# Up projections of three feed-forward stages as 2x2 block products with seven multiplications

## The chip, the cores and the metric

One core of one Trainium2 chip runs the whole program. The metric is the device time of one execution in microseconds (us). Three runs of the kernel before took 2185.04 to 2186.0 us, median 2185.47.

## What is computed

Input is one sequence of 512 tokens with 1024 features, float32 throughout. Two hybrid layers (attention, convolution and retention side by side) are followed by a third block with differential attention and a state space layer. Each of the three ends in a feed-forward stage, and only these three stages change:

```python
# hybrid layer, twice: w_up is 1024 x 4096, w_down 4096 x 1024
h = rms_norm(x, g_mlp_pre)
f = jnp.square(jax.nn.relu(h @ w_up)) @ w_down
return x + rms_norm(f, g_mlp_post)

# second block: w_up is 1024 x 5632 (gate and value), w_down 2816 x 1024
hn = rmsnorm(h, norm2_gain[i])
up = causal_dwconv(hn @ w_up[i], conv_w[i], conv_b[i])     # 3 taps along the tokens
gate, val = jnp.split(up, 2, axis=-1)
h = h + (jax.nn.silu(gate) * val) @ w_down[i]
```

## The kernel before

Every float32 operand of a matmul is split into a high part (rounded to the matmul's float32r type) and a low part, the remainder, and every product is three matmuls: high by high, high by low, low by high (mm3, L863, for up projections; t_part, L911, for down projections). A matmul contracts 128 rows and has a 128x128 stationary operand and up to 512 moving columns.

Weights are streamed (class Stream, L729) in chunks of 128x1024 in the order that stream_spec (L60) lists. A chunk is loaded by a DMA on SP's queue into one of NR = 4 raw buffers (wraw, pool wr). prep_to (L748) casts it to whi and subtracts to get wlo, each in one of NW = 4 buffers (pools wh and wl). The cast may go to ACT or DVE, the subtraction to DVE or POOL. The rest of SBUF is a pool sp of 79 - 2*NR - 4*NW = 55 tiles of 128x512 (L829). PSUM has two pools of four banks, psp and pss (L832, L833).

An up unit (f_unit, L890) makes 128 features for all 512 tokens: 8 blocks of the contraction, 24 matmuls of 512 columns into one bank. The input is the transposed, normed activation, hhi and hlo (to_hT, L985). The first four units of a stage go through f_split (L896): first the 256 columns of tokens 0 to 255 of all four, then the other 256, while the last token tiles are still being normed and transposed (mid_start, L1049). After a unit its evacuation runs: relu squared and a split into fhi and flo in mlp (relu2, L1454), the three-tap convolution on ACT and DVE, SiLU, gate times value and a split in ffn2 (unit, L2012). The down projection of four such units (down, L1483) is 96 matmuls of 512 columns, and DVE adds each bank to an accumulator tile (acc in mlp; in ffn2 the residual X itself). mlp (L1444) has 8 groups of four units; ffn2 (L2006) has 22 pairs of a gate and a value unit, four pairs to a down projection. finish_mlp (L1504) does the last down projection, the norm, the residual and the first half of the next stage's norm.

The order of the instructions is not the program's. Class Trace (L400) records every instruction with a due time and a cost by a formula (cost, L682), and order (L443) puts them on the engines' queues as a list schedule: each engine takes the ready instruction that is due first, up to WINDOW = 25160 ns ahead, if buffers are free (room, L609). Weight chunks are due PREPV = 15000 ns ahead of their use, evacuations EVV = 5000 ns ahead of the end of their unit. Where an instruction may go to two engines, a bias decides: Trace.sub (L648) passes an index into BIAS (L404), and POOL's end is counted as that many ns later. wbias is 2 (-4449 ns, in favour of POOL) outside the feed-forward stages and 3 (-1000 ns) in them; the index 1 means 100000 ns, so that POOL is never taken. The queues' order is fixed when the program is built.

Beside mlp of the first layer a side task (ssm_params, L1525) computes tables of the state space layer, mostly on POOL, and stores them.

Of the kernel before, what the change touches and what calls it, by code (L numbers as in the profile page):

```python
# [17 lines left out]
P = 128  # L18
# [28 lines left out]
def mlp_groups():  # L47
    return [(4 * g, 4) for g in range(NG1)]


def ffn2_groups():
    n = DFF2 // 128
    return [(k, min(4, n - k)) for k in range(0, n, 4)]
# [6 lines left out]
def stream_spec():  # L60
    out = []
    for l in range(LAYERS):
# [12 lines left out]
        gs = mlp_groups()  # L75
        for g, (k0, n) in enumerate(gs):
            out += [f_chunk("w_up", l, 128 * (k0 + i)) for i in range(n)]
            if g:
                out += down_chunks("w_down", l, *gs[g - 1])
        out += down_chunks("w_down", l, *gs[-1])  # L80
# [19 lines left out]
    gs = ffn2_groups()  # L100
    for g, (k0, n) in enumerate(gs):
        for i in range(n):
            out.append(f_chunk("w_up_2", 0, 128 * (k0 + i)))
            out.append(f_chunk("w_up_2", 0, DFF2 + 128 * (k0 + i)))
        if g:
            out += down_chunks("w_down_2", 0, *gs[g - 1])
    out += down_chunks("w_down_2", 0, *gs[-1])
# [117 lines left out]
class View:  # L225
    """A view of a tile that is traced before the tile is placed."""
# [103 lines left out]
class DramView(View):  # L330
    """A view of a tile in DRAM: taken as a whole."""
# [20 lines left out]
class Pool:  # L352
    """Equal slots, which the order of instructions deals out to tiles. Each is a pool of one buffer."""
# [46 lines left out]
class Trace:  # L400
    """Records instructions with the time by which each is wanted, orders them, and issues them."""
# [246 lines left out]
    def sub(self, out, a, b, bias=1):  # L648
# [3 lines left out]
        return self.add(alts, (out, a, b), {"op": ALU.subtract})  # L652
# [119 lines left out]

class Side:
# [35 lines left out]
class Builder:  # L809
# [3 lines left out]
    NR, NW = 4, 4  # L813
# [6 lines left out]
    def __init__(self, tc, ctx, A, out):  # L820
# [17 lines left out]
        self.wbias = 2  # L838

# [23 lines left out]
    def mm3(self, ps, w, a, start, stop):  # L863
        nc = self.nc
        (whi, wlo), (ahi, alo) = w, a
        nc.tensor.matmul(ps, whi, ahi, start=start, stop=False)
        nc.tensor.matmul(ps, whi, alo, start=False, stop=False)
        nc.tensor.matmul(ps, wlo, ahi, start=False, stop=stop)
        self.tick(3 * ahi.n * 0.422)
# [72 lines left out]
    # ---------------------------------------------------------------- norms  # L942
# [42 lines left out]
    def to_hT(self, t, hs):  # L985
        nc = self.nc
        for h in range(2):
# [4 lines left out]
            self.split(ps.rearrange("p (k n) -> p k n", k=4), self.hhi[sl], self.hlo[sl])  # L992
# [66 lines left out]
    # ---------------------------------------------------------------- attention helpers  # L1059
# [41 lines left out]
    def v_pack(self, src):  # L1101
        """V of six heads, each as 64 columns of high parts and 64 of low parts."""
# [11 lines left out]
    def pv_pair(self, h, pts, V, y):  # L1114
        """One head's output, from the products with the high and the low parts of V below each other."""
# [19 lines left out]
    def rows(self, third):  # L1135
        """Room for the four rows of blocks of a lower triangle."""
# [3 lines left out]
    def p_split(self, parts):  # L1140
        """High and low parts by blocks of keys: 512, 384 and twice 256 columns, the last with a block of zeros."""
# [58 lines left out]
    # ---------------------------------------------------------------- conv module  # L1200
# [48 lines left out]
    # ---------------------------------------------------------------- retention  # L1249
# [87 lines left out]
    # ---------------------------------------------------------------- hybrid layer  # L1337
    def hybrid(self, l):
# [69 lines left out]
        # output projection and residual  # L1408
# [14 lines left out]
        self.side.drain()  # L1423
        self.finish(lambda t: (p0[t],), 4, W_OUT_KS, mix, X, gpost, gpre)
# [18 lines left out]
    # ---------------------------------------------------------------- MLP  # L1443
    def mlp(self, l, X):  # L1444
        nc = self.nc
        groups = mlp_groups()
        self.wbias = 3
        if l == 0:
            self.side.add(self.ssm_params())
        acc = [None] * NT  # L1450
        f = {}
        last_g = len(groups) - 1

        def relu2(m):  # L1454
            def ev(ps):
                r = self.s2()
                nc.vector.tensor_scalar(r, ps, 0.0, None, op0=ALU.max)
                hi, lo = self.s2(F32R, "fhi"), self.s2(F32R, "flo")
                nc.scalar.activation(hi, r, AF.Square)
                nc.scalar.activation(r, r, AF.Square)  # L1460
                nc.vector.tensor_tensor(lo, r, hi.bitcast(F32), op=ALU.subtract)
                f[m] = (hi, lo)
            return ev
        lhs = lambda k, t0, t1: tuple(z[:, t0:t1] for z in f[k])
        for g, (k0, n) in enumerate(groups):
            if g == 0:
                self.f_split([relu2(i) for i in range(n)], self.mid_start((1, 3)))
                gpost = self.load_gain(4 * l + 3)
                nxt = 4 * (l + 1) if l + 1 < LAYERS else 8
                gpre = self.load_gain(nxt)  # L1470
            else:
                for i in range(n):
                    self.f_unit(relu2(k0 + i))
                self.down(groups[g - 1], lhs, acc, f, g == 1)
        xd = [[self.dp.tile(F32, f"xd{l}_{t}_{h}", [P, 512]) for h in range(2)] for t in range(NT)]

        def store(t):
            for h in range(2):
                nc.sync.dma_start(out=xd[t][h], in_=X[t][h])
        self.finish_mlp(groups[-1], lhs, acc, X, gpost, gpre, store)  # L1480
        self.xd = xd

    def down(self, grp, lhs, acc, f, first):  # L1483
# [20 lines left out]
    def finish_mlp(self, grp, lhs, acc, X, gpost, gpre, store):  # L1504
        nc = self.nc
        k0, n = grp
        nch = n // 2
        ks = list(range(k0, k0 + n))
        ws = [self.ws.take() for _ in range(2 * nch)]
        hs = {}  # L1510
        for t in range(NT):
            for h in range(2):
                ps = self.ps()
# [7 lines left out]
            store(t)  # L1521
        self.pending = hs

    # ---------------------------------------------------------------- SSM parameters
# [158 lines left out]
    # ---------------------------------------------------------------- SSM  # L1683
# [84 lines left out]
    # ---------------------------------------------------------------- differential attention  # L1768
# [84 lines left out]
    def second(self):  # L1853
# [139 lines left out]
        hs = {}  # L1993
        for t in range(NT):
# [11 lines left out]
    def ffn2(self, X):  # L2006
        nc = self.nc
        f, tg = {}, {}
        self.wbias = 3
        cw, cb = PV["convw2"][0], PV["convb2"][0]  # L2010

        def unit(i, val):  # L2012
            c = i + (22 if val else 0)

            def ev(ps):
                t = self.s2(name="cv")
                w = [self.pvt[:, cw + 3 * c + j:cw + 3 * c + j + 1] for j in range(3)]
                nc.scalar.activation(t, ps, AF.Identity, scale=w[2], bias=self.pvt[:, cb + c:cb + c + 1])
# [61 lines left out]
```

## Time and profile before

| | before |
|---|---|
| runs | 2185.04, 2185.47, 2186.0 us |
| span of the profiled execution | 2185.0 us |
| feed-forward stage of layer 0 (290 to 666) | 376 us |
| feed-forward stage of layer 1 (947 to 1305) | 358 us |
| feed-forward stage of the second block (1812 to the end) | 373 us |
| the rest | 1078 us |

The page gives no time of the profiled execution apart from its span, which lies within 0.05 us of the fastest run. Nearly every instruction carries the line 642, where the recorded instructions are issued, so the profile is read by the names of tiles: wraw, whi and wlo are weights, hhi and hlo the input of the up projections, fhi and flo the input of the down projections, ps a PSUM bank, acc or X an accumulator, cv a convolved unit. The duration of a matmul in the trace is longer than the distance from one start to the next, since matmuls overlap; the distance of starts is what counts. The same holds for DVE and ACT to a lesser degree.

### The profile page before, as it was taken

What the parts mean: (1) busy time and instruction counts of PE and PEld (TensorE: products, weight loads), DVE (VectorE), ACT (ScalarE), POOL (GpSimd) and SP (SyncE); (2) the same over time, 40 slices, a digit from 0 to 9 for tenths busy, and PEclk for the clock granted to TensorE, in tenths of its full rate; (3) what the DMA queues carried; (4) which work ended last, traced back from release to release, by engine and by line L of the source; (5) the groups of instructions that cost most, each with busy time, mean ns of one, the idle gap of its engine ahead of it and who ended that gap; (6) DMA issues with size and microseconds to landing.
All of it is one profiled execution on the core that took longest, in us unless ns stands there. A gap on an engine that the chain in (4) does not pass through costs nothing. (4 is left out here: it accounts for less than half of the span.)

```text
span 2185.0 us, 27033 instructions
## 1 busy us (share of the span) xinstructions
PE 2065.8 (95%) x9964; PEld 1711.6 (78%) x9964; DVE 1395.2 (64%) x2131; ACT 928.5 (42%) x1521; POOL 745.5 (34%) x858
## 2 busy tenths in 40 slices
PE   7789989899999799989999998999999999999999
PEld 7777878778888777788888877677777788888887
DVE  6999596344457999573444464379888646655545
ACT  3267544232234267454222344456578324433332
POOL 3663357980004663210000115764643431000000
PEclk9999999999999999999999999999999999999999
DMA  5223233332333224133332346222224533333222
GB/s 176 80 78 123 87 116 109 128 127 87 97 114 97 87 68 135 49 107 97 96 97 77 115 133 201 79 80 68 92 82 135 169 96 97 97 96 97 87 87 77
DMA packets 85556, 225.16 MB, mean 103 GB/s; under 512 B 10416, under 2 KB 20400, under 8 KB 85424
## 3 DMA queue, kind: packets, MB, share of 16 engines
q1 hardware_dynamic: 85424, 223.43, 32.4%
q8 instruction: 79, 1.29, 0.3%
q14 instruction: 53, 0.43, 0.1%
HBM read 204.25 MB, written 19.14 MB: 102 GB/s over the span
## 5 line engine op out<-in xcount | busy, mean ns | idle before, releaser
L642 POOL TENSOR_TENSOR wlo<-wraw,whi 128x1024 fp32r<-128x1024 f32 (+1 forms) x156 | 374.5, 2408 | 1068.3 <-ACT whi L642 824.9
L642 ACT CAST whi<-wraw 128x1024 fp32r<-128x1024 f32 (+1 forms) x323 | 330.4, 1029 | 726.7 <-PE ps L642 592.1
L642 PE MATMUL ps<-hhi,whi 128*128 128x512 f32 (+1 forms) x1488 | 506.8, 370 | 7.3 <-DVE acc L642 3.1
L642 PE MATMUL ps<-hlo,whi 128*128 128x512 f32 (+1 forms) x1488 | 504.8, 370 | 5.6 <-DVE hlo L642 5.6
L642 PE MATMUL ps<-hhi,wlo 128*128 128x512 f32 (+1 forms) x1488 | 504.3, 369 | 0.3 <-DVE wlo L642 0.3
L642 PEld LDWEIGHTS ps<-hhi,whi 128*128 128x128 f32 x1488 | 272.4, 191 | 54.8 <-issue 4.0
L642 PEld LDWEIGHTS ps<-hlo,whi 128*128 128x128 f32 x1488 | 272.4, 191 | 53.5 <-DVE hlo L642 6.8
L642 PEld LDWEIGHTS ps<-hhi,wlo 128*128 128x128 f32 x1488 | 272.1, 191 | 48.2 <-DVE wlo L642 1.0
L642 DVE TENSOR_TENSOR wlo<-wraw,whi 128x1024 fp32r<-128x1024 f32 x178 | 223.4, 1257 | 114.8 <-ACT whi L642 114.5
L642 PE MATMUL ps<-whi,fhi 128*128 128x512 f32 x688 | 249.7, 392 | 6.1 <-DVE t L642 3.7
L642 PE MATMUL ps<-whi,flo 128*128 128x512 f32 x688 | 249.5, 391 | 0.0
L642 PE MATMUL ps<-wlo,fhi 128*128 128x512 f32 x688 | 249.5, 391 | 0.0
L642 PE MATMUL ps<-wlo,hhi 128*128 128x384 f32 (+1 forms) x448 | 162.7, 380 | 18.3 <-POOL wlo L642 18.1
L642 DVE TENSOR_TENSOR acc<-ps,acc 128x512 f32<-128x512 f32 x112 | 76.5, 687 | 154.7 <-PE ps L642 154.7
L642 PE MATMUL ps<-whi,hhi 128*128 128x384 f32 (+1 forms) x448 | 161.7, 383 | 14.2 <-DVE rotb L642 12.7
L642 PE MATMUL ps<-whi,hlo 128*128 128x384 f32 (+1 forms) x448 | 158.8, 377 | 0.0
L642 PEld LDWEIGHTS ps<-whi,fhi 128*128 128x128 f32 x688 | 129.6, 189 | 34.7 <-DVE t L642 4.2
L642 PEld LDWEIGHTS ps<-wlo,fhi 128*128 128x128 f32 x688 | 129.6, 189 | 27.8
L642 PEld LDWEIGHTS ps<-whi,flo 128*128 128x128 f32 x688 | 129.5, 188 | 27.8
L642 DVE SCALAR_TENSOR_TENSOR cacc<-cy,pv,cacc 128x509 f32<-128x509 f32 (+26 forms) x120 | 125.3, 1088 | 0.6
L642 POOL TENSOR_TENSOR st<-st,mhalf 128x1 f32<-128x1 f32 (+1 forms) x56 | 54.9, 981 | 194.4 <-DVE st L642 190.8
L642 PEld LDWEIGHTS ps<-wlo,hhi 128*128 128x128 f32 x448 | 86.9, 195 | 30.6 <-POOL wlo L642 21.6
(250 smaller groups left out, 3167.8 us busy)
## 6 DMA issues: line engine op xcount, KB each, us to landing
wraw<-in_wst SPq DMA_DIRECT2D x302, 512.0 KB, 3.5
wraw<-in_wst SPq DMA_DIRECT2D x32, 384.0 KB, 3.1
gain<-in_gains SPq DMA_DIRECT2D x20, 256.0 KB, 4.2
X<-in_x SPq DMA_DIRECT2D x16, 256.0 KB, 6.1
xd<-X SPq DMA_DIRECT2D x16, 256.0 KB, 2.0
X<-xd SPq DMA_DIRECT2D x16, 256.0 KB, 4.9
gated<-t SPq DMA_DIRECT2D x16, 256.0 KB, 2.4
gate<-gated SPq DMA_DIRECT2D x16, 256.0 KB, 3.7
```

The lines of the kernel that those rows point to most:

```text
L642: getattr(getattr(self.nc, e), m)(*[r(x) for x in op.args], **{k: r(v) for k, v in op.kw.items()})
```

## The change

In each feed-forward stage the first group of f_split stays as it is (four units). All further up units are taken in pairs: two units in mlp (14 pairs for each layer), a gate and a value unit in ffn2 (20 pairs). Such a pair is a product of a 1024x256 weight with a 1024x512 activation, cut into 2x2 blocks: the contraction in halves of 512, the features in 128 and 128, the tokens in 256 and 256. In place of eight block products there are seven, of sums and differences of blocks (the form by Winograd). A block product is 4 x 3 = 12 matmuls of 256 columns, a pair 84 of them, where two units were 48 of 512.

What belongs to it: the weight sums are formed from the two raw chunks of a pair and then split (take_fast); the activation sums are formed once for a stage from copies of the transposed input (to_hT with rawT, fast_in), and one of them takes the place of a quarter of hhi and hlo; seven block products accumulate in two banks of psp, and after each, or nearly, ACT copies or DVE adds the bank out of PSUM (FastUp.out). The products 4 and 3 of a pair run amid the next pair or the next down projection (fast_unit, fast_end). Activation functions then read SBUF. Down projections take their banks from pss. mlp stores the residual X in DRAM at its start and loads it again tile by tile at its end. The order of the weight stream follows. In these stages wbias is 1. NW is 5, so sp has 51 tiles. The diff is cut to its core:

```diff
-    NR, NW = 4, 4
+    NR, NW = 4, 5
+    PROD = 1300
...
+    def take_fast(self):            # class Stream
+        b, nc = self.b, self.b.nc
+        j = self.next_use
+        self.load_to(j + 2)
+        x, y = self.raw.pop(j), self.raw.pop(j + 1)
+        self.next_prep = self.next_use = j + 2
+        t0 = b.T - b.PREPV
+        L, R = slice(0, 512), slice(512, 1024)
+        out = {}
+        def split(src, names):
+            if len(names) == 2:
+                hi, lo = b.wh.tile(name="whi"), b.wl.tile(name="wlo")
+            else:
+                hi, lo = b.s2(F32R, "whi"), b.s2(F32R, "wlo")
+            nc.copy(hi, src)
+            nc.sub(lo, src, hi.bitcast(F32), b.wbias)
+            for i, n in enumerate(names):
+                out[n] = hi[:, 512 * i:512 * i + 512], lo[:, 512 * i:512 * i + 512]
+        b.prio(t0)
+        split(x, (1, 2))
+        b.prio(t0 + 3 * b.PROD)
+        z, z4 = b.wr.tile(name="wsum"), b.s2(name="wsum")
+        nc.sum(z[:, L], x[:, L], y[:, L], b.wbias)
+        nc.sum(z[:, R], z[:, L], y[:, R], b.wbias)
+        split(z, (5, 6))
+        b.prio(t0 + 6 * b.PROD)
+        nc.sum(y[:, L], y[:, L], y[:, R], b.wbias)
+        nc.sum(z4, z[:, R], x[:, R], b.wbias)
+        split(y, (7, 3))
+        b.prio(t0 + 8 * b.PROD)
+        split(z4, (4,))
...
+class Fast:
+    FIRST = {1, 2, 5}
+    def run(self, i):
+        self.mm(i, self.pa if i in (1, 6, 7, 4) else self.pb, i in self.FIRST)
+        self.b.evac(self.out, i)
+class FastUp(Fast):
+    def mm(self, i, ps, first):
+        whi, wlo = (x.rearrange("p (k m) -> p k m", k=4) for x in self.w.pop(i))
+        for k in range(4):
+            self.b.mm3(ps[:, :256], (whi[:, k, :], wlo[:, k, :]), self.a(i, k), first and k == 0, k == 3, ...)
+    def out(self, i):
+        if i == 1:
+            nc.copy(m0[:, L], pa)
+        elif i == 2:
+            nc.vector.tensor_tensor(g0[:, L], pb, m0[:, L], op=ALU.add)
+        elif i == 6:
+            nc.copy(m0[:, R], pa)
+        elif i == 7:
+            nc.copy(m1[:, L], pa)
+            nc.vector.tensor_tensor(g1[:, R], pb, m1[:, L], op=ALU.subtract)
+        elif i == 4:
+            nc.copy(g0[:, R], pa)
+            self.done(0, g0)
+        elif i == 3:
+            nc.vector.tensor_tensor(g1[:, L], pb, m0[:, R], op=ALU.subtract)
+            self.done(1, g1)
...
             self.split(pv, self.hhi[sl], self.hlo[sl])          # to_hT
+            if self.rawT is not None:
+                for j in range(2):
+                    ...
+                    nc.copy(r[:, :, (t % 2) * P:(t % 2 + 1) * P], pv[:, 2 * j:2 * j + 2, :])
+    def fast_in(self):
+        for j in range(2):
+            s1, s2, s4, s3 = (self.s2(name="sraw") for _ in range(4))
+            nc.sub(s1, R[1, j], R[1, j + 2], self.wbias)
+            nc.sub(s2, s1, R[0, j], self.wbias)
+            nc.sum(s4, R[0, j + 2], s2, self.wbias)
+            nc.sub(s3, R[0, j], R[1, j], self.wbias)
+            for i, s in ((6, s2), (5, s1), (3, s4)):
+                hi, lo = self.s2(F32R, "shi"), self.s2(F32R, "slo")
+                nc.copy(hi, s)
+                nc.sub(lo, s, hi.bitcast(F32), self.wbias)
+            hi, lo = (z[:, 2 * j:2 * j + 2, 256:512] for z in (self.hhi, self.hlo))
+            nc.copy(hi, v)                                       # v is s3
+            nc.sub(lo, v, hi.bitcast(F32), self.wbias)
+    def fast_unit(self, u):
+        v = self.before
+        for i in (1, 2, -4, 6, -3, 5, 7):                        # minus: of the pair before
+            if i > 0:
+                u.run(i)
+            elif v:
+                v.run(-i)
+        self.before = u
...
 def mlp(self, l, X):
-        self.wbias = 3
+        self.wbias = 1
+        xm = self.spill(X, f"xm{l}")
+        self.f_split([relu2(i) for i in range(4)], self.mid_start((1, 3)))
+        a = self.fast_in()
+        for kind, i in mlp_plan():                               # up 2, down 0, up 3, up 4, down 1, ...
             if kind == "up":
+                self.fast_unit(FastUp(self, self.ws.take_fast(), a, done(i)))
             else:
+                self.down((4 * i, 4), lhs, acc, f, i == 0)
 def down(self, grp, lhs, acc, f, first):
-                ps = self.ps()
+                ps = self.ps(side=True)
+                if h == 0 and t < 2:
+                    self.fast_end((4, 3)[t:t + 1])
 def ffn2(self, X):
-        self.wbias = 3
+        self.wbias = 1
-            nc.vector.tensor_tensor(t, t, g, op=ALU.mult)
+            nc.sub(t, t, tg.pop(i), self.wbias, ALU.mult)
+        for kind, i in ffn2_plan():                              # up 2, 3, 4, down 0, up 5 to 8, down 1, ...
             if kind == "up":
+                self.fast_unit(FastUp(self, self.ws.take_fast(), a, lambda e, g, i=i: conv(i, e, g)))
             else:
+                self.down((4 * i, 4), lhs, X, f, False)
```

## Rows read from the trace of the kernel before

**Rows 1.** The page: span, and busy time and share of each engine.
```profile
span 2185.0 us, 27033 instructions
PE 2065.8 (95%) x9964; PEld 1711.6 (78%) x9964; DVE 1395.2 (64%) x2131; ACT 928.5 (42%) x1521; POOL 745.5 (34%) x858
```

**Rows 2.** Windows over the three feed-forward stages: start and end, length, then busy us and number of instructions of PE, PEld, DVE, ACT and POOL, the granted clock of TensorE as a share of full speed, the DMA share and GB/s.
```profile
290.00:666.00 376.00, 362.68 (x1652) 298.58 (x1653) 202.55 (x340) 119.57 (x166) 169.77 (x373) 0.98 0.35 109
947.00:1305.00 358.00, 357.09 (x1655) 296.21 (x1654) 176.26 (x225) 121.18 (x169) 22.54 (x17) 1.00 0.33 100
1812.00:2185.00 373.00, 368.69 (x1699) 303.73 (x1697) 204.25 (x249) 125.57 (x160) 17.72 (x8) 1.00 0.29 92
```

**Rows 3.** The chain of work that ended last: start, us, what.
```profile
1819.57 361.70 PE ps L642 x1640
```

**Rows 4.** Waits of PE in the stage 290 to 666: who waited for whom, us in total, times, longest.
```profile
PE ps L642 <- DVE t L642: 4.5, 3, 3.7
PE ps L642 <- DVE acc L642: 4.2, 2, 2.4
PE ps L642 <- DVE hlo L642: 4.0, 2, 2.4
```

**Rows 5.** POOL in order of time between 1060 and 1300 (start, us, engine, line, operation, tiles): one weight chunk in each group of four up units and one down projection.
```profile
1069.18 2.71 POOL L642 TENSOR_TENSOR wlo<-wraw,whi 128x1024 fp32r<-128x1024 f32 x1 [41.48 <-ACT whi L642]
...
1245.93 2.65 POOL L642 TENSOR_TENSOR wlo<-wraw,whi 128x1024 fp32r<-128x1024 f32 x1 [41.51 <-ACT whi L642]
```

**Rows 6.** PE in order of time in a stretch of up matmuls of 256 columns, in f_split of the second stage: the first and the last of 13.
```profile
962.14 0.28 PE L642 MATMUL ps<-hhi,whi 128*128 128x256 f32 x1
...
963.50 0.28 PE L642 MATMUL ps<-hhi,whi 128*128 128x256 f32 x1
```

**Rows 7.** Windows of dense stretches, PE alone: busy us, number of matmuls that touch the stretch (one or two more than start in it), granted clock, DMA share, GB/s. The first three hold matmuls of 512 columns, the last two of 256.
```profile
1040.00:1060.00 20.00, 20.00 (x90) 1.00 0.30 97
2000.00:2020.00 20.00, 20.00 (x87) 1.00 0.44 136
2100.00:2120.00 20.00, 20.00 (x90) 1.00 0.30 83
312.00:320.00 8.00, 8.00 (x73) 1.00 0.21 49
1832.00:1837.00 5.00, 5.00 (x45) 1.00 0.57 125
```

**Rows 8.** PE in order of time at the start of the first feed-forward stage, 256 columns: a wait, and matmuls after it.
```profile
293.19 0.58 PE L642 MATMUL ps<-hlo,whi 128*128 128x256 f32 x1 [2.40 <-DVE hlo L642]
...
294.00 0.41 PE L642 MATMUL ps<-hlo,whi 128*128 128x256 f32 x1
294.21 0.41 PE L642 MATMUL ps<-hhi,wlo 128*128 128x256 f32 x1
...
296.13 0.41 PE L642 MATMUL ps<-hhi,wlo 128*128 128x256 f32 x1
```

**Rows 9.** Groups of DVE instructions in the last stage (1812 to 2185): tiles, shapes, number | busy us, mean ns of one | idle time before them.
```profile
L642 DVE TENSOR_TENSOR wlo<-wraw,whi 128x1024 fp32r<-128x1024 f32 x57 | 71.3, 1253 | 77.3 <-ACT whi L642 77.1
L642 DVE TENSOR_TENSOR X<-ps,X 128x512 f32<-128x512 f32 x49 | 33.7, 688 | 69.3 <-PE ps L642 69.1
L642 DVE SCALAR_TENSOR_TENSOR cv<-ps,pv,cv 128x510 f32<-128x510 f32 x44 | 32.8, 748 | 1.5
L642 DVE TENSOR_TENSOR flo<-cv,fhi 128x512 fp32r<-128x512 f32 x22 | 15.2, 692 | 14.4 <-ACT fhi L642 14.4
```

**Rows 10.** Groups of DVE instructions in the second stage (947 to 1305), the same columns.
```profile
L642 DVE TENSOR_TENSOR wlo<-wraw,whi 128x1024 fp32r<-128x1024 f32 x55 | 67.2, 1222 | 20.5 <-ACT whi L642 20.5
L642 DVE TENSOR_SCALAR t<-ps 128x512 f32<-128x512 f32 x32 | 22.1, 691 | 61.9 <-PE ps L642 61.8
```

**Rows 11.** DVE in order of time, 1068 to 1074, beside the first POOL chunk of rows 5.
```profile
1070.33 2.12 DVE L642 TENSOR_TENSOR flo<-t,fhi 128x512 fp32r<-128x512 f32 x1 [0.71 <-ACT t L642]
1072.37 0.68 DVE L642 TENSOR_TENSOR acc<-ps,acc 128x512 f32<-128x512 f32 x1
1072.97 1.21 DVE L642 TENSOR_TENSOR wlo<-wraw,whi 128x1024 fp32r<-128x1024 f32 x1
```

**Rows 12.** DVE in order of time, 1982 to 1984: a weight subtraction and the instruction right behind it.
```profile
1982.02 1.22 DVE L642 TENSOR_TENSOR wlo<-wraw,whi 128x1024 fp32r<-128x1024 f32 x1 [1.08 <-ACT whi L642]
1983.16 0.68 DVE L642 TENSOR_TENSOR X<-ps,X 128x512 f32<-128x512 f32 x1
```

**Rows 13.** Groups of ACT and DVE instructions over the whole span, by shape: a weight cast, ACT copies out of PSUM of 512 and 384 columns, and a DVE subtraction with one operand in PSUM, of 384 columns.
```profile
L642 ACT CAST whi<-wraw 128x1024 fp32r<-128x1024 f32 x291 | 304.0, 1051 | 647.1 <-PE ps L642 535.5 <-DVE X L642 61.1 <-issue 37.6
L642 ACT CAST hhi<-ps 128x512 fp32r<-128x512 f32 x48 | 27.3, 585 | 38.9 <-PE ps L642 38.4
L642 ACT CAST pthi<-ps 128x384 fp32r<-128x384 f32 x52 | 23.7, 490 | 3.5 <-PE ps L642 2.8 <-PE o L642 0.3
L642 DVE TENSOR_TENSOR ptlo<-ps,pthi 128x384 fp32r<-128x384 f32 x52 | 27.0, 545 | 0.8 <-ACT pthi L642 0.7
```

**Rows 14.** Weight loads of TensorE over the whole span.
```profile
L642 PEld LDWEIGHTS ps<-hhi,whi 128*128 128x128 f32 x1488 | 272.4, 191 | 54.8 <-issue 4.0 <-ACT hhi L642 2.6 <-DVE acc L642 1.4
```

**Rows 15.** DMA issues: size, median us from issue to landing.
```profile
wraw<-in_wst SPq DMA_DIRECT2D x302, 512.0 KB, 3.5
xd<-X SPq DMA_DIRECT2D x16, 256.0 KB, 2.0
X<-xd SPq DMA_DIRECT2D x16, 256.0 KB, 4.9
```

**Rows 16.** Waits of PE over the whole span: the two longest in total.
```profile
PE ps L642 <- DVE t L642: 20.5, 14, 3.7
PE ps L642 <- POOL wlo L642: 18.1, 6, 7.2
```

More of the change, by code (lines that the diff above doesn't have):

```diff
@@ L44, with mlp_plan, ffn2_plan @@
 W_OUT_KS = (3, 4, 0, 1, 5, 6, 7, 2)
[L47 to L53, printed above, removed]
+NF2 = DFF2 // 128
+def mlp_plan():
+    out = []
+    for g in range(NG1 - 1):
+        last = g == NG1 - 2
+        out.append(("up", 2 * g + 2))
+        if last:
+            out.append(("up", 2 * g + 3))
+        out.append(("down", g))
+        if not last:
+            out.append(("up", 2 * g + 3))
+    return out
+def ffn2_plan():
+    out = [("up", 2), ("up", 3)]
+    n = NF2 // 4
+    for g in range(n):
+        i = 4 * g + 4
+        out.append(("up", i))
+        if g == n - 1:
+            out.append(("up", i + 1))
+        out.append(("down", g))
+        if g < n - 1:
+            out += [("up", i + e) for e in range(1, 4)]
+    return out
 GATES = (2, 3, 4, 7)
@@ L99, in stream_spec @@
         out += t_chunks("w_out_2", 0, ((512 * h, 512),))
[L100 to L107, printed above, removed]
+    up2 = lambda i: [f_chunk("w_up_2", 0, DFF2 * e + 128 * i) for e in range(2)]
+    out += up2(0) + up2(1)
+    for kind, i in ffn2_plan():
+        out += up2(i) if kind == "up" else down_chunks("w_down_2", 0, 4 * i, 4)
+    out += down_chunks("w_down_2", 0, NF2 - 2, 2)
     return out
@@ new lines, with __init__ @@
+class Fast:
+    FIRST = {1, 2, 5}
+    def __init__(self, b, w, a):
+        self.b, self.w, self.a = b, w, a
+        self.pa, self.pb = b.ps(), b.ps()
+    def run(self, i):
+        self.mm(i, self.pa if i in (1, 6, 7, 4) else self.pb, i in self.FIRST)
+        self.b.evac(self.out, i)
+        if i in (2, 3):
+            self.pb = self.pb if i == 2 else None
+class FastUp(Fast):
+    def __init__(self, b, w, a, done):
+        super().__init__(b, w, a)
+        self.done = done
+        self.g = [b.s2(name="cu") for _ in range(2)]
+        self.m = [b.s2(name="mid") for _ in range(2)]
+    def mm(self, i, ps, first):
+        whi, wlo = (x.rearrange("p (k m) -> p k m", k=4) for x in self.w.pop(i))
+        for k in range(4):
+            self.b.mm3(ps[:, :256], (whi[:, k, :], wlo[:, k, :]), self.a(i, k), first and k == 0, k == 3,
+                       skip_group_check=not first)
+    def out(self, i):
+        nc, (g0, g1), (m0, m1) = self.b.nc, self.g, self.m
+        pa, pb = self.pa[:, :256], self.pb[:, :256]
+        L, R = slice(0, 256), slice(256, 512)
+        if i == 1:
[13 more added lines that the diff above has]
+            self.done(1, g1)
@@ L838, in __init__ @@
         self.wbias = 2
+        self.rawT = None
+        self.before = None
     def s2(self, dt=F32, name="t"):
@@ L994, in run, with fast_end @@
+    def fast_unit(self, u):
[6 more added lines that the diff above has]
+        self.before = u
+    def fast_end(self, steps=(4, 3)):
+        if self.before:
+            for i in steps:
+                self.before.run(i)
+            if 3 in steps:
+                self.before = None
     def run(self):
@@ L1441, in finish, with spill @@
         self.pending = hs
+    def spill(self, X, name):
+        out = [[self.dp.tile(F32, f"{name}_{t}_{h}", [P, 512]) for h in range(2)] for t in range(NT)]
+        for t in range(NT):
+            for h in range(2):
+                self.nc.sync.dma_start(out=out[t][h], in_=X[t][h])
+        return out
     def mlp(self, l, X):
         nc = self.nc
-        groups = mlp_groups()
-        self.wbias = 3
+        self.wbias = 1
         if l == 0:
             self.side.add(self.ssm_params())
-        acc = [None] * NT
@@ L1457, in ev @@
                 nc.vector.tensor_scalar(r, ps, 0.0, None, op0=ALU.max)
[L1458 to L1462, printed above, removed]
-            return ev
-        lhs = lambda k, t0, t1: tuple(z[:, t0:t1] for z in f[k])
[L1465 to L1470, printed above, removed]
-            else:
-                for i in range(n):
-                    self.f_unit(relu2(k0 + i))
-                self.down(groups[g - 1], lhs, acc, f, g == 1)
+                finished(m, r)
@@ L1993, in second @@
         hs = {}
+        self.rawT = {}
         for t in range(NT):
@@ new lines, in conv @@
+            if not val:
+                nc.scalar.activation(t, t, AF.Silu)
+                tg[i] = t
+                return
+            nc.sub(t, t, tg.pop(i), self.wbias, ALU.mult)
+            hi, lo = self.s2(F32R, "fhi"), self.s2(F32R, "flo")
+            nc.copy(hi, t)
+            nc.sub(lo, t, hi.bitcast(F32), self.wbias)
+            f[i] = hi, lo
+        us = [lambda ps, i=i, v=v: conv(i, v, ps) for i in range(2) for v in (False, True)]
+        self.f_split(us, self.mid_start((1, 3)))
```

136 lines of the change are left out of this document (83 added, 53 removed).

## The prediction

> **What bounds the kernel now.** The page first: PE is busy 95% of the span, DVE 64%, ACT 42% [rows 1]. A share can mislead, so the windows come next: in the three feed-forward stages PE is busy 363 of 376, 357 of 358 and 369 of 373 us, while DVE has 203, 176 and 204 us, ACT about 122 each and POOL, apart from the parameter task of the first stage, next to nothing [rows 2]. The chain of waits says the same from the other side: the last 362 us are one unbroken piece of PE [rows 3]. In the first stage PE waits for DVE some 13 us [rows 4], in the others hardly at all. So these stages last as long as their matmuls, and fewer columns make them shorter until another engine is as long.
>
> What a matmul costs there is the distance of starts. The POOL chunk that recurs once in each group of 192 matmuls of 512 columns gives (1245.93 - 1069.18) / 4 = 44.19 us a group [rows 5], 0.230 us a matmul; dense windows give 0.226 to 0.234 [rows 7]. With 256 columns 12 steps take 1.36 us, 0.113 us each [rows 6], and windows 0.112 to 0.116 [rows 7]. Half the columns cost half the time; a fixed cost per matmul doesn't show.
>
> **What is removed on PE.** A pair of units was 48 x 0.230 = 11.04 us and becomes 84 matmuls at half of 0.230, 9.66 us: 1.38 us less. With 14 + 14 + 20 = 48 pairs that is **-66 us**. With 0.113 to 0.118 for the short matmul it lies between -54 and -75. It is all on PE, which sets the end.
>
> Here a rule speaks against the change. Each short matmul still has a 128x128 weight load of its own, of 191 ns [rows 14], longer than the 113 ns to the next matmul; the dense rows [rows 6, 7] show that the loads overlap well enough at 256 columns, in the same form of matmul. The Trainium skill, "TensorE: Matmul & The Clock Gate", section "Back-to-back issue gap", gives for streams of weight loads and matmuls 81 ns at 128 columns and 131 ns at 512; drawn as a line between, an estimate of mine, 256 columns would cost 98 ns, a pair 8.2 us for 6.3, and the sum would be +92 us in place of -66. The trace doesn't agree with the page: 512 columns take 230 ns here, not 131 [rows 7]. By the rows the short matmul is half the long one, and the sum goes by them.
>
> **What is added on DVE and ACT.** A subtraction of 1024 columns takes DVE 1.22 us, one of 512 0.69 [rows 9, 10]; back to back the next starts after 1.14 [rows 12] and 0.60 [rows 11], so both prices are bounds. For a pair the weights were two subtractions of 1024; they become three of 1024, one of 512 and four sums of 512: 7.1 us for 2.4 by durations (6.4 for 2.3 by starts). Out of PSUM come three additions of 256 columns; from 0.69 at 512 and 0.545 at 384 [rows 9, 13] an estimate is 0.40 each, 1.2. The stage's subtractions that POOL did (about one in eight [rows 5]) come on top, 8 us a stage, and fast_in is 16 instructions of 512, 10 to 11 us. The convolution or the relu costs what it did.
> - ffn2: 204 + 20 x 5.9 + 8 + 11 = **341 us** of DVE by durations; by starts, 20 x 5.1 + 8 + 10, 324. PE's stage becomes 373 - 27.6 = 345. The cover is nearly used up.
> - mlp of layer 1: 176 + 14 x 5.4 + 19 = 271 of 339 us (a relu that reads SBUF I count half a microsecond cheaper for the pair). Layer 0: about 298 of 357.
> - ACT: a pair has 3.5 casts for 2, +1.6 us [rows 13], and four copies of 256 columns, estimated at 0.39 from 0.585 and 0.490 [rows 13], 1.6: some +64 us in ffn2 on 126 [rows 2]. It stays half idle and hides this.
>
> **Where that reaches PE.** Four places.
> 1. *The start of each stage.* The products 6, 5, 7, 4 and 3 need fast_in, which needs the last transposed tile. From then PE has the second halves of f_split, 4 x 24 x 0.113 = 10.9 us, and the products 1 and 2, 2.8 us. DVE has in these 13.7 us four evacuations (some 5 us), the first pair's weights (6.4), of which one buffer's worth can be ready before, and for product 6 at least s1, s2 and two subtractions for each half, 4.8 us: 15 to 16 us. A wait of some us also drops the clock: after the 2.4 us wait the matmuls were 0.21 apart for 3 us, the lower of the two levels (1.2 for 2.4 GHz) [rows 8]. I take 4 us a stage, between 0 (products of the next pair fill in) and 11 (all of fast_in in the open): **+12**, 0 to 33.
> 2. *ffn2 in its middle.* Four pairs are 38.6 us of PE and, with weights and convolution, some 45 to 50 of DVE; the down projection after them is 22 of PE and some 10 of DVE. DVE falls behind and catches up. A convolved unit has a pair's time of slack before its down projection. I take **+14**; 0 if the slack is enough, 35 if DVE (341 by durations) and its waits set the stage.
> 3. *The first stage.* POOL's parameter task runs on. A DVE subtraction took 2.12 in place of 0.69 us while POOL was at work on a chunk [rows 5, 11], and PE waited there for DVE 4.5 + 4.2 us [rows 4], with DVE half idle. At 83% I take **+6**, 0 to 15. Taking the weights from POOL removes such meetings in the two others.
> 4. *Everything else.* NW = 5 lets one weight chunk more be ready; PE's waits for POOL's chunks, 18.1 us [rows 16], could shrink. Four tiles fewer in sp narrow how far the schedule runs ahead, and the whole order is dealt anew. I take 0, -10 to +10.
>
> Queues. On SP's queue mlp issues 16 DMAs more per layer: the stores of X (2.0 us each) and the loads at the end (4.9) [rows 15], ordered among weight loads with tens of us to spare; I take nothing. The cover is the 44 us group; without it one load, 4.9 us, lands on the end of the stage. A weight load waits until its raw buffer is free, and a pair now holds three of the four (two chunks and a sum), the last until DVE has made the sum for product 4; the next loads, and any store behind them on SP, wait with it. Landing (3.5) and three dependent sums (0.69 each and a 1.2 us instruction ahead of each) make a round of about 9.2 us against 9.66 of PE: enough, with little to spare in ffn2; its price is inside the 0 to 35 of place 2. On PE, the first matmul of products 6, 7 and 4 waits until ACT has copied the bank out, of 5 and 3 until DVE has added it; whatever is queued behind on PE, down projections included, waits too. Two products or more lie between, 2.8 us against a copy of 0.4, so I take nothing and keep the price for a rival.
>
> Sum: -66 + 12 + 14 + 6 = -34. From the span of 2185.0 that is **2151 us**. The execution stands at the fastest of the runs, 0.5 under their median; nothing need be added.
>
> **Rivals.**
> - *DVE becomes the bound of ffn2 and takes its whole gain* (for it: 341 of 345 us by durations, and a pair's 11 to 12 us of DVE against 9.66 of PE; against it: 324 by starts, and down projections to catch up in). Then only the two mlp stages gain, 38.6 us, less 8 for their starts, 6 for the first stage and some 4 for DVE's waits in them: **2164**. Chance 0.18.
> - *Slower: the hand-over of banks.* Each of 48 x 7 = 336 products needs its bank emptied by an engine that also does everything else in a fixed order; PE takes no other work past a matmul that waits. Forecast gain 34 us / 336: from 0.10 us of wait a product on, the change loses. For it: DVE behind by one delayed instruction of 2.12 us [rows 11] delays the banks of two products, and PE already waits longest for DVE, 20.5 us in 14 waits [rows 16]. Against it: 2.8 us between uses, and ACT half idle. At 0.2 us a product it costs 67 us: 2151 + 67 = **2218**. Chance 0.17.
> - *The short matmul pays for its load.* If loads of 191 ns [rows 14] followed one another without overlap, a pair would be 84 x 0.191 = 16.0 us, 5 more than before: +238 us, **2423**. Rows 6 and 7 show the overlap over dozens of matmuls, so chance 0.02. The page's own line, above, would come to 2277.
>
> **How the numbers follow.** The forecast has 0.63. This measurement can tell about 0.2%, 4.4 us, from no change. The forecast and the first rival lie under 2181 but for some 0.05 to 0.07 of their 0.81; the rivals on the other side make 0.19. So faster 0.76, same 0.05, slower 0.19. The terms' own bounds run from 2100 to beyond 2200 if all go one way; the forecast's own range is 2125 to 2175. To leave out no more than 2 in 10 the range takes in the first rival and the nearer part of the second: **2120 to 2196**.
>
> **What would show it.** Right: in the profile after, some 4032 matmuls of 256 columns in pairs, 0.113 to 0.118 apart; DVE above 90% busy in ffn2 and about 80% in mlp; stages of about 367, 343 and 363 us; PE's waits in them on DVE's shi, slo and whi tiles near the start. The first rival: PE waits on wlo or flo all through ffn2, that stage near 373. The second: hundreds of short waits of PE for g0, g1 or m tiles. Wrong: short matmuls further apart than 0.12 at full clock, or a change outside the three stages by over 10 us.

## The result and the profile after

The changed kernel takes 2198.4 us (median; 2197.6 to 2201.4), the kernel before 2185.3: a ratio of 1.0064, 95% interval 1.0050 to 1.0078. It is **slower by 13 us**, where 34 us faster was forecast; the range ended at 2196.

The page of the profile after, which answers to [rows 1]:

```profile
span 2196.0 us, 31375 instructions
PE 2025.7 (92%) x11692; PEld 1767.2 (80%) x11692; DVE 1662.4 (76%) x2639; ACT 1090.6 (50%) x1883; POOL 715.8 (33%) x836
```

PE has 40 us less to do, and the span is 11 us longer. The windows of the three stages, with the columns of [rows 2], tell two stories:

```profile
300.00:696.50 396.50, 355.35 (x2166) 319.49 (x2167) 286.41 (x496) 166.97 (x277) 182.42 (x367) 0.94 0.35 116
988.60:1332.70 344.10, 341.08 (x2168) 309.22 (x2166) 247.54 (x374) 167.78 (x277) 9.07 (x12) 1.00 0.35 118
1840.20:2196.00 355.80, 344.83 (x2419) 319.01 (x2417) 309.70 (x451) 190.03 (x299) 0.93 (x1) 1.00 0.28 95
```

The second and third stage are still PE's, though DVE is busy 72% and 87% of them. The first is not: PE stands idle for 41 us, and its granted clock is 0.94. For a table by parts each part is cut at the last matmul with wlo of the projection before it, so that the parts add up to the span (us, from the traces):

| | layer 0, up to its feed-forward stage | feed-forward 0 | layer 1 | feed-forward 1 | second block | its feed-forward | median time |
|---|---|---|---|---|---|---|---|
| before | 287 | 379 | 276 | 363 | 507 | 373 | 2185.3 |
| after | 300 | 397 | 292 | 344 | 507 | 356 | 2198.4 |
| difference | +13 | +18 | +16 | -18 | 0 | -17 | |

In the changed kernel one or two matmuls with whi follow that cut by up to 5.6 us, behind transposes for the next part. Cut behind them, the differences of the first five parts would be +13, +22, +12, -14 and -4: a few us can be counted to either neighbour, and the two stories stay.

So the change does in two stages what it was to do. It loses in the first stage, and **in two parts of the program that it doesn't touch**.

The short matmuls are about as far apart as [rows 6] had them, 0.11 to 0.12 us. In the second stage, in order of time:

```profile
1099.76 0.28 PE L662 MATMUL ps<-hhi,whi 128*128 128x256 f32 x1
1099.88 0.28 PE L662 MATMUL ps<-hlo,whi 128*128 128x256 f32 x1
1099.99 0.28 PE L662 MATMUL ps<-hhi,wlo 128*128 128x256 f32 x1
1100.10 0.28 PE L662 MATMUL ps<-slo,whi 128*128 128x256 f32 x1
```

The chain of work that ended last was one piece of PE of 362 us in the last stage [rows 3]. There it now breaks once in each round of four pairs and a down projection, every 62.8 us: 52.3 us are one piece of PE, and most of the rest runs over DVE's cv, wlo and wsum (three rounds; start, us, what):

```profile
1952.73 52.26 PE ps L662 x356
2015.49 52.28 PE ps L662 x356
2078.26 52.28 PE ps L662 x356
```

Where PE waits in the first stage (who for whom, us, times, longest), against [rows 4]:

```profile
PE ps L662 <- DVE cu L662: 28.8, 4, 14.8
PE ps L662 <- ACT mid L662: 5.0, 1, 5.0
PE ps L662 <- DVE t L662: 3.3, 2, 2.8
```

Four waits for cu, the tile into which DVE adds a bank. What holds DVE up shows in its own waits and in those of SP's queue in that stage. The kernel before had them too, and the prediction did not look: it asked who PE waits for, and not what waits stand in the queues ahead of that. Before, DVE then SP:

```profile
DVE t L642 <- POOL t L642: 48.0, 8, 9.4
SPq L642 <- POOL t L642: 86.9, 16, 13.2
```

After:

```profile
DVE t L662 <- POOL t L662: 40.2, 8, 9.0
SPq L662 <- POOL t L662: 107.3, 14, 17.5
```

DVE stands 40 us behind POOL, eight times, each time at an instruction that puts a sign on a finished table of the parameter task. In the kernel before, with DVE half idle, these waits and SP's together cost the stage some 8 us (e8_before_fix below). Now the bank of a product is behind them. DVE in order of time, 482 to 492:

```profile
482.03 0.07 DVE L662 MEMSET t<- 128x4 f32 x2
491.15 0.50 DVE L662 TENSOR_SCALAR t<-t,pv 128x512 f32<-128x512 f32 x1 [9.05 <-POOL t L662]
491.58 0.68 DVE L662 TENSOR_TENSOR acc<-ps,acc 128x512 f32<-128x512 f32 x1
492.18 0.41 DVE L662 TENSOR_TENSOR cu<-ps,mid 128x256 f32<-128x256 f32 x1
```

PE waited 7.1 us for that cu, till 492.6. The longest wait, 14.8 us till 384.6, has no such instruction before it. There DVE works off 69 small operations of the parameter task in one row, from 365.3 to 384.1. The new order put them there: in the kernel before at most 19 of them stand in a row in this stage. Many are long where POOL reads SBUF at the same time. DVE, and POOL beside it:

```profile
372.21 0.18 DVE L662 COPY prm<-prm 128x32 f32<-128x32 f32 x1
372.42 1.00 DVE L662 TENSOR_TENSOR prm<-prm 128x32 f32<-128x32 f32 x1
```
```profile
372.32 1.06 POOL L662 TENSOR_TENSOR t<-sbc,prm 128x512 f32<-128x512 f32 x1 [0.67 <-DVE prm L662]
```

The wait costs PE more than its length. For the 4.5 us behind it TensorE was granted half its clock; PE in order of time, and that window with the columns of [rows 2]:

```profile
384.56 0.58 PE L662 MATMUL ps<-shi,whi 128*128 128x256 f32 x1 [14.78 <-DVE cu L662]
...
386.65 0.41 PE L662 MATMUL ps<-shi,whi 128*128 128x256 f32 x1
386.86 0.41 PE L662 MATMUL ps<-slo,whi 128*128 128x256 f32 x1
```
```profile
384.50:389.00 4.50, 4.43 (x19) 4.24 (x20) 4.43 (x10) 0.59 (x1) 4.34 (x7) 0.50 0.13 28
```

### The profile page after: what moved, and what is told of

The parts are those of the page before. It is cut to its first block, busy times and chain, and to the rows that moved or that the text cites. A ratio compares the mean times of both kernels' runs of the same rounds, so it can differ in the third digit from the quotient of the medians.

```text
span 2196.0 us, 31375 instructions
## 1 busy us (share of the span) xinstructions
PE 2025.7 (92%) x11692; PEld 1767.2 (80%) x11692; DVE 1662.4 (76%) x2639; ACT 1090.6 (50%) x1883; POOL 715.8 (33%) x836
## 5 line engine op out<-in xcount | busy, mean ns | idle before, releaser
L662 POOL TENSOR_TENSOR wlo<-wraw,whi 128x1024 fp32r<-128x1024 f32 (+1 forms) x134 | 318.1, 2382 | 525.5 <-ACT whi L662 403.4
L662 ACT CAST whi<-wraw 128x1024 fp32r<-128x1024 f32 (+1 forms) x318 | 325.0, 1029 | 288.4 <-PE ps L662 229.0
L662 PE MATMUL ps<-hhi,whi 128*128 128x256 f32 (+1 forms) x1488 | 424.0, 313 | 9.1 <-ACT mid L662 6.1
L662 PE MATMUL ps<-hlo,whi 128*128 128x256 f32 (+1 forms) x1488 | 422.3, 312 | 7.7 <-DVE hlo L662 7.7
L662 PE MATMUL ps<-hhi,wlo 128*128 128x256 f32 (+1 forms) x1488 | 419.1, 310 | 1.5 <-DVE wlo L662 1.5
L662 DVE TENSOR_TENSOR wlo<-wraw,whi 128x1024 fp32r<-128x1024 f32 x200 | 247.5, 1245 | 40.1 <-ACT whi L662 39.9
L662 PE MATMUL ps<-shi,whi 128*128 128x256 f32 (+1 forms) x608 | 170.8, 293 | 32.6 <-DVE cu L662 28.8
L662 PE MATMUL ps<-wlo,hhi 128*128 128x384 f32 (+1 forms) x448 | 160.6, 383 | 15.6 <-POOL wlo L662 15.6
L662 PE MATMUL ps<-shi,wlo 128*128 128x256 f32 (+1 forms) x608 | 169.9, 291 | 0.0
L662 PE MATMUL ps<-slo,whi 128*128 128x256 f32 (+1 forms) x608 | 169.7, 290 | 0.0
L662 ACT COPY mid<-ps 128x256 f32<-128x256 f32 x144 | 52.7, 368 | 234.3 <-PE ps L662 232.5
```

The costliest lines, as they stand in the source:

```text
L662: getattr(getattr(self.nc, e), m)(*[r(x) for x in op.args], **{k: r(v) for k, v in op.kw.items()})
```

## Experiments

Twelve kernels ran, each against the kernel before on the same chip. Ratios are to it, with 95% intervals. Times are medians; the parts are those of the table above, from the one execution that was profiled, which can lie some us off the median. Every edit has the queues' order dealt anew, in all parts.

**Buffers alone, in the kernel before.** Three kernels without any of the change's code:

```diff
-    NR, NW = 4, 4
+    NR, NW = 4, 5                  # e1_before_nw5: sp has 51 tiles
-        self.sp = pool("sp", 79 - 2 * self.NR - 4 * self.NW, [P, 512])
+        self.sp = pool("sp", 75 - 2 * self.NR - 4 * self.NW, [P, 512])   # e2_before_sp51: 51 tiles, NW = 4
+        self.sp = pool("sp", 77 - 2 * self.NR - 4 * self.NW, [P, 512])   # e12_before_sp53: 53 tiles, NW = 4
```

> The kernel before with NW = 5 and so 51 tiles in sp, nothing else. Theory A (the buffers' sizes cost the 29 us by which the two attention, convolution and retention parts of layers 0 and 1 grew, 287 to 300 and 276 to 292 us): those two parts take about 300 and 292 us here too, the feed-forward stages stay at 379, 362 and 373, and the time is about 2212. Rival B (the change's own code deals the order anew there, sizes or not): both parts stay at 287 and 276 and the time at 2185, within 5.

Measured 2220.7 us, ratio 1.0164 (1.0147 to 1.0181). Parts 302, 379, 291, 365, 505, 373. As theory A said, the two parts grow and the feed-forward stages hardly do; the time is 9 us above what it gave.

> The kernel before with 51 tiles in sp, NW = 4 kept (four tiles lie unused). Theory A1 (it is the four tiles of sp that are missing): about 2212, the parts of layers 0 and 1 at 300 and 292 us. Theory A2 (it is the fifth weight buffer, which lets more chunks go ahead of other work): 2185 within 5, both parts at 287 and 276.

Measured 2207.2 us, 1.0101 (1.0085 to 1.0116). Parts 302, 379, 292, 361, 500, 373. Theory A1 holds: four tiles fewer in sp, otherwise unused, lengthen the same two parts by 15 and 16 us. By the medians of the two runs the fifth weight buffer, with 51 tiles in both, makes the kernel before 13 us slower, not faster; by the profiled executions it is 7. Windows over the first part, before and in e2_before_sp51, columns as in [rows 2]:

```profile
0.00:287.30 287.30, 248.31 (x1309) 216.71 (x1310) 233.66 (x387) 144.55 (x273) 134.92 (x142) 0.96 0.34 112
```
```profile
0.00:302.30 302.30, 252.41 (x1309) 218.81 (x1310) 237.70 (x386) 147.03 (x275) 135.06 (x142) 0.94 0.32 105
```

The same work; PE stands 50 us idle for 39 and is granted less clock. Its waits in that part, before and in e2_before_sp51:

```profile
PE ps L642 <- DMA cm<-in_cmat: 8.0, 1, 8.0
PE ps L642 <- DVE t L642: 7.5, 4, 2.8
PE ps L642 <- DVE xlo L642: 2.1, 1, 2.1
PE ps L642 <- DVE row L642: 1.2, 2, 0.9
```
```profile
PE ps L642 <- DVE t L642: 16.0, 5, 7.6
PE ps L642 <- DVE row L642: 7.6, 5, 2.0
PE ps L642 <- DVE xlo L642: 5.6, 2, 5.4
PE ps L642 <- DVE stk L642: 5.0, 2, 3.8
```

The line for t is no growth: its longest wait, 7.6 us, is the one at the program's start, which the view of the kernel before puts down to the load of cm (8.0). What grew are row (attention), xlo and stk (mostly retention): 18.2 us, where row and xlo were 3.3 and stk had no wait.

> The kernel before with 53 tiles in sp, NW = 4. If each tile that is missing holds back a little (theory A1, gradual): the parts of layers 0 and 1 take about 294 and 284 us, the time is about 2196. If there is a step (some set of tiles fits or doesn't): 287 and 276 and 2185, or 302 and 292 and 2207.

Measured 2183.6 us, 0.9995 (0.9984 to 1.0006); parts 291, 378, 270, 362, 511, 373. Two tiles fewer cost nothing, four cost 22 us: a step. That it is no accident of one order shows over all kernels of this document: in the six with 51 tiles the two parts take 299 to 302 and 291 to 295 us, in the seven with 55 tiles 282 to 288 and 272 to 276. Which instruction finds no room at 51 was not traced and stays open.

**The changed kernel with NW = 4** and so 55 tiles in sp.

> The changed kernel with NW = 4 and so 55 tiles in sp. Theory A: the parts of layers 0 and 1 come back to about 287 and 276 us, a gain of 29; the feed-forward stages, which lose a weight buffer, lose 0 to 15 in exchange: 2170 to 2185. Rival B: both parts stay near 300 and 292 and the time at 2198 or above.

Measured **2172.1 us**, 0.9941 (0.9925 to 0.9957). Parts 282, 397, 272, 347, 507, 365. The parts of the two layers come back, even a little below the kernel before. With four weight buffers the second stage takes 3 us more and the last 9. The run changes buffers and tiles at once; that the tiles are what moves the two parts rests on e1 and e2. One line of the diff turns a loss of 13 us into a gain of 13.

**The first stage.** First the instruction on DVE that stands behind POOL is taken away, by giving the sign to the start value:

```diff
         ph = cmul(ph, ph, ph)
+        V.tensor_scalar(ph[1], ph[1], sgn, None, op0=ALU.mult)
...
-            V.tensor_scalar(Sn, Sn, sgn, None, op0=ALU.mult)
```

> The changed kernel, but the sign that DVE multiplies onto each finished sine table (8 times a DVE instruction that stands in DVE's queue and waits for POOL, 40 us in all) is put once onto the 128x32 start value, which gives the same tables. Theory C (PE's 28.8 us of waits for cu in the first feed-forward stage come from DVE standing behind POOL's tables): the five waits between 405 and 514 us (2.3, 4.6, 2.8, 7.1, 5.0) go, the one of 14.8 at 384 stays, that stage falls from 396 to about 376 and the time to about 2178. Rival D (DVE's two-input work and POOL's hold each other up, whoever waits in a queue): the stage keeps most of its waits, 390 or more, 2192 or more.

Measured 2194.0 us, 1.0038 (1.0023 to 1.0053); the stage 390 for 397. Theory C fell as it stood: DVE's eight waits are gone, and PE waits as long. What rival D gave, 390 or more and 2192 or more, came. The next thing that is late shows in SP's queue in order of time (start, time on the queue):

```profile
424.76 0.33 SPq L662 DMA_DIRECT2D std<-t  x1
425.13 0.43 SPq L662 DMA_DIRECT2D wraw<-in_wst  x1
441.81 0.32 SPq L662 DMA_DIRECT2D ctd<-t  x1
443.38 0.32 SPq L662 DMA_DIRECT2D std<-t  x1
443.80 1.83 SPq L662 DMA_DIRECT2D wraw<-in_wst  x4
```

The table's store holds the queue for 16 us until POOL has the table, and four weight loads go out behind it at once. SP's waits for POOL in this stage have grown from 107 to 138 us. ACT's cast waited for the load till 447.7, DVE's subtraction stood 8.2 us behind the cast, and the bank behind that: 8.7 us of PE. So the next run also moves the stores to POOL's own queue, here with NW = 4:

```diff
-            nc.sync.dma_start(out=self.ctd[b], in_=C)
-            nc.sync.dma_start(out=self.std[b], in_=Sn)
+            nc.gpsimd.dma_start(out=self.ctd[b], in_=C)
+            nc.gpsimd.dma_start(out=self.std[b], in_=Sn)
```

> The changed kernel with NW = 4, the sine's sign put on the start value, and the 16 table stores issued from POOL's own queue in place of SP's, all of the computation kept. Theory C2: with neither DVE nor the weight loads behind POOL, the first stage falls from 396.5 to 365 to 380 (the wait of some 8 to 15 us at the parameters' small operations stays, as does POOL's slowing of DVE), and the time to about 2145. Rival D2: 390 or more, 2165 or more.

Measured 2160.6 us, 0.9889 (0.9874 to 0.9904); the stage 384 for 397. It gains 11.5 us on the run with NW = 4 alone, all of it in that stage, but the result lies between theory and rival: the stage is 4 us above what theory C2 gave and the time 16, and both are below what rival D2 gave. The two queues together are thus worth 12 us. For scale, the whole of POOL's tables left out:

```diff
             V.memset(Cv[:, :, 0:1], 1.0)
             V.memset(Sv[:, :, 0:1], 0.0)
-            for j in range(7):     # six POOL operations each
...
+            V.memset(C, 1.0)
+            V.memset(Sn, 0.0)
+            yield 9000
```

> The changed kernel without POOL's 336 multiplications and additions that build the cosine and sine tables (the tables are filled with constants, so that part of the computation is left out); NW = 5. Theory C2 (in the first feed-forward stage PE loses to POOL's tables, on three ways: DVE waits for POOL in its queue, the table stores hold SP's queue and the weight loads behind them, and POOL's reads slow DVE): that stage falls from 396.5 to 355 to 366 us and the time to about 2162. Rival D2 (the stage is long because DVE has more to do there than it has time for, the parameters' small operations and the sums together): 385 or more.

Measured 2165.9 us, 0.9916 (0.9902 to 0.9931); the stage 364, as theory C2 gave. Of its 52 us above feed-forward 1 the tables make 32. How much of that is queues and how much is slower DVE work, no run separates; none moves the stores alone. One wait of 15.2 us at 385 is left, for cu. To tell whether those small operations are too many or are slowed, POOL's last work for the task went too, the 24 products and sums that combine the parameters:

```diff
-            nc.gpsimd.tensor_tensor(v3(o), v3(b), bc(a), op=ALU.mult)
-            nc.gpsimd.tensor_tensor(v3(t), v3(bp_), bc(ap_), op=ALU.mult)
-            nc.gpsimd.tensor_tensor(o, o, t, op=ALU.add)
-            nc.sync.dma_start(out=dst, in_=o)
+            nc.sync.dma_start(out=dst, in_=b)
```

> The changed kernel (NW = 5) without POOL's tables and without POOL's 24 products that combine the parameters (raw inputs are stored in their place), so that POOL has next to no work beside the first feed-forward stage, while DVE keeps all of its small parameter operations. Theory E (the wait of 15 us at 385 that was left without the tables is DVE's small operations made slow by POOL's reads: 0.3 us each and more for 0.1 to 0.2): the wait shrinks to 5 or less, the stage from 364 to about 351, the time to about 2152. Rival F (it is the number and the place of those operations in DVE's order): the wait stays at 10 or more, 2162 or more.

Measured 2146.8 us, 0.9831 (0.9814 to 0.9847); the stage **346**, like feed-forward 1 (344). Theory E holds, and the gain is larger than it gave. DVE's operations prm by prm in the stage, without the tables and without any of POOL's work for the task (number | busy us, mean ns):

```profile
L662 DVE TENSOR_TENSOR prm<-prm,prm 128x32 f32<-128x32 f32 x68 | 19.6, 310 | 0.3
```
```profile
L662 DVE TENSOR_TENSOR prm<-prm,prm 128x32 f32<-128x32 f32 x65 | 10.8, 189 | 0.4
```

and the two longest waits of PE that are left in it, without POOL's work:

```profile
PE ps L662 <- DVE hlo L662: 2.1, 1, 2.1
PE ps L662 <- ACT hhi L662: 0.8, 1, 0.8
```

The operations are as many as ever, and they still stand in one row. That row, DVE's operations on prm alone (window, length, busy us and number, granted clock, DMA share, GB/s), without the tables and without any of POOL's work for the task:

```profile
365.70:384.40 18.70, 17.38 (x65) 0.66 0.19 72
```
```profile
355.13:365.30 10.17, 8.79 (x70) 1.00 0.10 37
```

At half the time for the same row the wait of 15 us is gone, so their number and place, rival F, are not the cause by themselves. SP's queue no longer waits for POOL's products either (26 us in e5), so not all of the 18 us need be DVE's. The Trainium skill, "SBUF — State Buffer", section "Who interferes with whom", says that a DVE instruction with two inputs in SBUF contends with a GpSimd instruction that reads SBUF. The trace agrees: the operation of 372.42 took 1.00 us, where such operations without POOL take 0.19; it began 0.10 us into a POOL product of 1.06 and ended 0.04 us behind it.

**Versions.** The first stage left as before, NW = 4:

> NW = 4, the feed-forward stage of layer 0 as before, the other two with seven products. If the stages add up, it takes 284 + 379 + 274 + 347 + 507 + 362, about 2153. If a part after a plain first stage is laid out anew and loses, up to 2170.

Measured 2157.7 us, 0.9876 (0.9859 to 0.9892); parts 288, 378, 272, 347, 509, 363. They add up within 5 us. The kernel before with the sign and the stores changed as in e6_sign_poolq:

> The kernel before with the sign on the start value and the table stores on POOL's queue. Theory C2: there DVE also stood 48 us behind POOL's tables, but PE lost only some 9 us to it, so the first stage falls from 379 by 5 to 12 us and the time to about 2177. If the fix does nothing for PE here: 2185.

Measured 2178.0 us, 0.9970 (0.9957 to 0.9983); its first stage 371 for 379. So the fix is worth 8 us to that stage, and 6 to the whole. Both together:

> NW = 4, the first feed-forward stage as before but with the sine's sign on the start value and the table stores on POOL's queue, the other two with seven products. If the two gains add up (2157.7 less the 7 that the fix gave to the kernel before): about 2151. If the order that is dealt anew takes it back: up to 2160.

Measured 2159.8 us, 0.9886 (0.9872 to 0.9901); the first stage 380. They don't add up, and why the fix gains nothing there was not found. Last, all three stages with seven products, with the fix, and the parameter task spread out:

```diff
-            self.side.add(self.ssm_params())
+            self.side.add(self.ssm_params(), 30000)
...
-        yield 3000
+        yield 4500                 # each step of the task
```

> All three stages with seven products, NW = 4, sign and stores as in the run with POOL's queue, and the parameter task begun 30 us later and stretched by half (its steps due 4.5 us apart in place of 3). Theory E says that the small operations cost PE most where they come in a row beside POOL's products: further apart they fit between DVE's other work, the stage falls from 384 to 365 to 375, the time to about 2145. Rival F2 (the amount of DVE's and POOL's work in that stage sets it): 380 or more, 2157 or more.

Measured **2144.1 us**, 0.9811 (0.9797 to 0.9826), the whole computation kept; parts 283, 369, 272, 347, 508, 365. Stage and time are what theory E gave. In place of one row of 70 small operations (e6) the longest rows have 26 and 20. The tables' products are spread with them, so the run doesn't tell the two apart. It is the fastest here, 40 us under the kernel before and 54 under the changed one.

## Why the prediction was wrong

The step that failed is the pricing of what stands outside PE's own work, at two places: place 3, the parameter task beside the first stage, taken at +6 us, and place 4, everything else, taken at 0 with no price on the four tiles of sp.

- *PE's gain.* Right in the mechanism, and nearly in size. Short matmuls came 0.11 to 0.12 apart; feed-forward 1 fell by 18 us of 19.3 (14 by the later cut), the last by 17 of 27.6. The estimate from the Trainium skill ("TensorE: Matmul & The Clock Gate", "Back-to-back issue gap") and the rival of loads that don't overlap are out.
- *Place 1, the start of a stage.* +4 us each was too much: in the second stage PE waited 2.1 and 0.9 us, no more than in the kernel before at that place, and nowhere for fast_in. The lower bound was right.
- *Place 2, DVE in ffn2.* +14 against +10 by the table (17 gained of 27.6), the start included. DVE's durations in that stage add up to 342 us, as the 341 had it, but neighbours overlap by 32 us of it (5 before), and DVE is busy 310 us, below the 324 by starts too. The first rival is out.
- *Place 3, the first stage: the step that failed most.* +6, bounds 0 to 15, became +37 (from -19 to +18). The prediction priced POOL's slowing of DVE by PE's waits before, 8.7 us. It missed that DVE and SP, both in order, stood 48 and 87 us behind POOL in that stage already, that the change puts PE's banks behind them, and that the new order sets 69 of the task's small operations in one row. e5 and e9 show POOL's work as the cause: without the tables the stage is 32 us shorter, without the products too another 18. e6 prices the two queues at 12 us; the blocked reads are shown for the row at 385. How the rest divides stays open. Without POOL's work the stage takes 346 us, less than the 360 that PE's gain alone leaves of 379: POOL's work cost the kernel before, too.
- *Place 4, everything else: failed.* "I take 0, -10 to +10" became +29, and the prediction's own sign of being wrong, a change outside the three stages by over 10 us, came. The prediction named the four tiles and gave them no price; e2 prices them at 22 us in the kernel before, e3 at 26 in the changed one, less what the fifth weight buffer is worth there. The waits for POOL's chunks, which that buffer was to shorten, went from 18.1 to 15.6 us.
- *The rival of the bank hand-over* had the direction and the tile right, and the wrong picture: not hundreds of short waits but five long ones in one stage. In the second stage the hand-over cost nothing, in the last 2.6 us.

With the parts as measured, the sum is 2185 - 66 + 1 + 10 + 37 + 29 = 2196, the span of the profiled execution after; it must come out, since the sizes are read from the two spans. The prediction set the span of 2185.0 beside the times of runs and added nothing. The runs that have both show a time some 1.7 us above the span of the same execution (2197.7 and 2196.0 here), so its 2151 stands for a time of about 2153; beside 47 us that is small.

## What to carry to other kernels

Where an engine's busy share goes from about half to 72 or 87%, list that engine's and the DMA queue's own waits first: a wait that cost little then holds whatever the change queues behind it. Take buffers from a shared pool only after a run of the old kernel with the smaller pool; two tiles cost nothing here and four cost 22 us, in parts that the diff doesn't touch. A loss beside a real gain can be taken apart by stage: in two of three stages the change gained from the start.

## What the runs showed of the hardware

- A DVE operation of 128x32 elements with two inputs takes 0.19 us without POOL's work (e9) and took 1.00 beside a POOL product that reads SBUF. POOL's own table products (t from t and prm) went from 353 to 465 ns on average, where DVE was busy 286 us in the stage for 203.
- Matmuls of 256 columns, each with its own weight load of 0.19 us, run 0.114 us apart for some 150 in a row without a break, half the 0.230 us of 512 columns [rows 5].
- After the wait of 14.8 us the short matmuls are 0.21 us apart for 5 us: the granted clock is 0.50 there, the lower of the two levels, and 0.94 over the stage, where feed-forward 1 has 1.00.
- DMAs on SP's queue go out in its order: a store that waited 16 us for POOL's table held the weight loads behind it, and four went out at once when it was gone (e4).
